# Second-layer memory keys and values moved into the first layer's token-major z products

## The chip, the cores and the metric

The kernel runs on one core of one Trainium2 chip. The metric is the device time of one execution in microseconds (us); lower is better. A core has TensorE (PE: matmuls, and PEld for its weight loads), VectorE (DVE), ScalarE (ACT), GpSimd (POOL) and SyncE (SP), whose queue issues nearly all transfers of this kernel.

## The reference

Two decoder layers over a sequence of 1024 tokens of width 1024, then a final norm. Cut to what matters here:

```python
for l in range(DEPTH):                                   # DEPTH = 2
    h = rms_norm(x, norm_mix_w[l])
    x = x + hybrid_mixer(h, w_in[l], ...)                # one projection of h: q, k, v, gates, z, xbc, dt
    hq = rms_norm(x, norm_xq_w[l])
    mem_n = rms_norm(mem, norm_mem_w[l])                 # mem: 256 tokens, the same for both layers
    x = x + memory_cross_attention(hq, mem_n, w_mq[l], w_mk[l], w_mv[l], w_mo[l])
return rms_norm(x, final_norm_w)

# memory_cross_attention:
k = (mem_n @ wk).reshape(b, m, 4, 256)
v = (mem_n @ wv).reshape(b, m, 4, 256)
```

The keys and values of the memory depend on `mem` and on weights alone, not on `x`. They can be computed at any time before the cross-attention of their layer, which comes at the end of that layer.

## The kernel before

Activations lie feature-major in SBUF: `hhi` and `hlo` hold the normed input as 8 tiles of 128 features by 1024 tokens. Every fp32 operand is split into a high part (a rounded copy, made on ACT by `hi`, L77) and a low part (the rest, made by `lo`, L85, on DVE or POOL). A product is three matmuls, high by high, low by high and high by low (`mm3`, L111 to L113).

The order of PE's instructions is written by hand: PE executes them in the order in which the Python code emits them. The order on the other engines and in SP's queue of transfers is chosen when the program is built, from a model of times and with program order as priority; each queue is then executed in its order. `weave(main, fill)` (L297) emits two generators alternately. A generator yields its modelled PE time as a float; a tuple `(t,)` means "nothing of mine is to be emitted before model time t", and `weave` then emits `fill` until that time, as long as `fill` has anything left. `ratio` says how much of `fill` goes with each step of `main`; at 0.0 `fill` goes into the tuples alone.

The program begins in `start`. It computes memory keys and values of layer 0, `memkv(0)`, and of layer 1, `memkv(1)`, as the `fill` of `norms()`, which norms the memory and the 1024 tokens of x in two halves of 512. Each `memkv` is 8 key tiles (8 k-steps of three matmuls with 256 columns) and 4 pieces of values (2 token chunks of 8 such k-steps): 384 matmuls. Its weights come through `wload`, which loads 128x512 pieces and splits them, into two sets of buffers: `wp` (names `wst`, `whi`, `wlo`, five pieces) and the local pool `n0` (names `xst`, `xhi`, `xlo`, three pieces). `alt_w` decides whether every second low part is made on DVE or all of them on POOL. Results are scaled (`kf`), split (`kh`, `kl`) and stored to DRAM.

The norm of a half is a chain: 8 loads `xt`, squares on ACT (`nsq`), sums on DVE (`nac`, L265), 8 small matmuls that sum over partitions (L221), the reciprocal root (`nms`, `nrs` on POOL, `nrp`, `ndg`), two matmuls that spread it over partitions (L251), a copy `nrr`, and then 8 products `ntm` (L270, DVE) that are split into `hhi` and `hlo`. The eight `xt` buffers are reused by the second half, and `ntm` has three buffers.

What is left of `fill` after the norms is run in `tokmaj` as `first`, ahead of the token-major products: pieces 0 and 1 (v and small gates: `values(0)` for tokens of the first half, `values(1)` for those of the second), then `gate_z`: pieces 2, 3 and 4 (z), 8 token chunks each, woven into `gates`. A piece's weights are loaded in four pairs of k-tiles (`tms`, three buffers), and split on ACT (`tmh`) and POOL (`tml`). Its matmuls are L372 to L374. The pool `tm` with these buffers is opened on the right side of SBUF after the pool `n1` of the norms (`xt`, `nsq`, `nac`, `nrr`, `ntm`, `ndg`, `wn`) was closed there, so its buffers take over addresses of those tiles, and a buffer is first written when the old tiles under it have been read for the last time. After `tokmaj` comes `mixer`, whose first projection loads its weights (`in_w_fm`) through `wp` too.

Of the kernel before, what the change touches and what calls it, by code (L numbers as in the profile page):

```python
# [8 lines left out]
F32 = mybir.dt.float32  # L9
F32R = mybir.dt.float32r  # L10
# [6 lines left out]
P = 128  # L17
# [3 lines left out]
KT = D // P  # L21
NB = T // P
HALF = 512
MT = 256
# [19 lines left out]
class Net:  # L44
# [300 lines left out]
    def tokmaj(self, l, pools, first, norm):  # L345
        nc = self.nc
        mm = nc.tensor.matmul
        W = max(PIECES)
        with self.pool("tm", 2, side="right") as pool:
            self.fdt = self.tile(pool, [P, NB, 24], F32, "fdt", 1)  # L350
            ws = {}
# [44 lines left out]
            def values(half):  # L396
                for pc in range(2):
                    for c in range(4 * half, 4 * half + 4):
                        yield from run(pc, c)

            def gate_z():
                for pc in range(2, len(PIECES)):
                    load(pc)
                    for c in range(NB):
                        yield from run(pc, c)
# [7 lines left out]
            if l == 0:  # L413
                self.fixed_rows()
            self.run(values(1))
            self.weave(self.gates(l), gate_z())


    def gates(self, l):
# [769 lines left out]
    def memnorm(self, pool, tmp):  # L1189
        nc = self.nc  # L1190
        mt = self.mt
        nch = MT // P
        sums = []
        for k in range(0, KT, 2):
            sq = [self.tile(tmp, [P, MT], F32, "msq", 8) for _ in range(2)]
            nc.scalar.activation(sq[0], mt[:, k, :], AF.Square)
            nc.gpsimd.tensor_tensor(out=sq[1], in0=mt[:, k + 1, :], in1=mt[:, k + 1, :], op=ALU.mult)
            nc.vector.tensor_tensor(out=sq[0], in0=sq[0], in1=sq[1], op=ALU.add)
            sums.append(sq[0])
        ps = self.tp()  # L1200
        for c in range(nch):
            for k, sq in enumerate(sums):
                nc.tensor.matmul(
                    ps[:, c : c + 1], sq[:, c * P : (c + 1) * P], self.onecol, start=k == 0, stop=k == len(sums) - 1
                )
        self.mrr = yield from self.spread(tmp, ps, nch, self.tile(pool, [P, MT], F32, "mrr", 1))
        self.mrs = self.const("mrs", [P, nch])
        nc.vector.tensor_copy(self.mrs, self.rs[:, :nch])

    def memw(self, l, pool):  # L1210
        w = self.mw[l]
        if l == 0:

            nhi, nlo = (h[:, :, HALF : HALF + MT] for h in (self.hhi, self.hlo))
        else:
            nhi, nlo = (self.tile(pool, [P, KT, MT], F32R, n, 1) for n in ("nhi", "nlo"))
        for k in range(KT):
            self.hi(nhi[:, k, :], self.mt[:, k, :], w[:, k : k + 1])
            self.lo(nlo[:, k, :], self.mt[:, k, :], nhi[:, k, :], w[:, k : k + 1])
        return nhi, nlo  # L1220


    def memkv(self, l, pool, w0):
        nc, a = self.nc, self.a
        mm = nc.tensor.matmul
        nhi, nlo = self.memw(l, pool) if l == 0 else self.mnext
        todo = []

        def acc(i):
            return self.acc() if i % 2 else self.big()  # L1230

        def keys(t, ps):
            kf = self.tile(pool, [P, MT], F32, "kf")
            nc.vector.tensor_tensor(out=kf, in0=ps, in1=self.mrr, op=ALU.mult)
            kh = self.tile(pool, [P, MT], F32R, "kh")
            kl = self.tile(pool, [P, MT], F32R, "kl")
            self.hi(kh, kf)
            self.lo(kl, kf, kh, eng=nc.gpsimd)
            self.dma(self.kDs[l][0][:, t, :], kh)
            self.dma(self.kDs[l][1][:, t, :], kl)  # L1240

        def values(pc, c, ps):
            r = self.mrs[:, c : c + 1]
            vh = self.tile(pool, [P, MT], F32R, "kh")
            vl = self.tile(pool, [P, MT], F32R, "kl")
            self.hi(vh, ps, r)
            self.lo(vl, ps, vh, r)
            self.dma(self.mvDs[l][0][:, c, pc * MT : (pc + 1) * MT], vh)
            self.dma(self.mvDs[l][1][:, c, pc * MT : (pc + 1) * MT], vl)
# [5 lines left out]
                g(*b)  # L1255

        for t in range(KT):
            ws = w0[t] if t < len(w0) else self.wload(a["w_mk"][l, t], (None, pool)[t % 2])
            ps = acc(t)[:, :MT]
            for k in range(KT):  # L1260
                whi, wlo = ws[k // 4]
                s = slice((k % 4) * P, (k % 4 + 1) * P)
                self.mm3(ps, whi[:, s], wlo[:, s], nhi[:, k, :], nlo[:, k, :], k == 0, k == KT - 1)
                yield 0.33
            put(keys, t, ps)
# [3 lines left out]
        for pc in range(4):  # L1269
            ws = self.wload(a["w_mv"][l, pc, 0]) + self.wload(a["w_mv"][l, pc, 1], pool)  # L1270
            for c in range(2):
                ps = acc(c)[:, :MT]
# [221 lines left out]
    def start(self):  # L1494
        a = self.a
        pools, xp = ExitStack(), ExitStack()
        pool = pools.enter_context(self.pool("n0", 2))
        xp_ = xp.enter_context(self.pool("n1", 2, side="right"))
        self.nb = 3
# [2 lines left out]
        nc = self.nc  # L1502
        nc.scalar.dma_start(self.mw[0], a["norm_mem_w"][0])
        w0 = [self.wload(a["w_mk"][0, 0], first=self.mt[:, 0:2, :])]
# [23 lines left out]
                yield from self.norm_half(xp_, xs, accs, wn, half)  # L1528

        self.ratio = 0.0  # L1530
        fill = chain(self.memkv(0, pool, w0), self.memkv(1, pool, []))
        self.weave(norms(), fill, drain=False)
        xp.close()
        return pools, fill, iter(())
# [84 lines left out]
```

## Time and profile before

| what | value |
|---|---|
| time, median of 3 runs | 2637.05 us (2633.95 to 2640.07) |
| the profiled execution, its own time | 2644.48 us |
| its span | 2642.7 us |
| PE busy | 2527.8 us, 96% of the span |
| DVE, ACT, POOL busy | 1590.9, 1219.2, 1085.6 us |
| mean granted clock of PE | 0.981 |
| share of the chain that ended last | PE 76%, DVE 9%, DMA 5% |

The page of the profile cuts the span in 40 slices of 66 us. These are the digits of busy time in tenths, and what the transfers moved:

```profile
PE   8799999999999988999999999999999998899997
PEclk9899999999999999999999999999999999999999
DMA  7673232222323745454364222222322465445333
GB/s 239 213 228 96 69 91 67 81 79 84 87 79 103 255 157 168 144 167 122 122 195 122 73 77 84 87 73 75 98 73 76 130 240 167 143 156 164 123 95 129
```

The first two slices are where PE has its lowest digits at the front of the program, and the first three where the transfers are densest. A row of the timeline reads: start in us, duration in us, engine, line, operation, output and inputs, shapes, and in brackets the idle time before it with what ended that. Durations of single matmuls overlap, since matmuls are pipelined; the pace is the distance from start to start.

### The profile page before, as it was taken

How to read it: one execution, taken by the hardware profiler on the slowest of the kernel's cores; microseconds unless marked ns; L12 is line 12 of the kernel's file. 1: busy time of each engine (PE TensorE's matmuls, PEld its weight loads, DVE VectorE, ACT ScalarE, POOL GpSimd, SP SyncE). 2: the span in 40 equal slices, each digit the busy share in tenths (PEclk: the TensorE clock that was granted, in tenths of full speed). 3: DMA queues.
4: the chain of work that ended last, by engine and by line, in shares of the span. 5: the costliest groups of instructions: out<-in, count | busy, mean ns of one | idle time of the engine just before them, and what ended most of it. 6: DMA issues, size and time to landing. Idle time of an engine off the chain costs nothing.

```text
span 2642.7 us, 39668 instructions
## 1 busy us (share of the span) xinstructions
PE 2527.8 (96%) x13900; PEld 2098.6 (79%) x13900; DVE 1590.9 (60%) x2940; ACT 1219.2 (46%) x2615; POOL 1085.6 (41%) x1081
## 2 busy tenths in 40 slices
PE   8799999999999988999999999999999998899997
PEld 7799988888777766778879988888877766577886
DVE  6823266666688666663464236666678867665445
ACT  5532254554466545534443135455455644443442
POOL 5642244444455544332252124344354555433233
PEclk9899999999999999999999999999999999999999
DMA  7673232222323745454364222222322465445333
GB/s 239 213 228 96 69 91 67 81 79 84 87 79 103 255 157 168 144 167 122 122 195 122 73 77 84 87 73 75 98 73 76 130 240 167 143 156 164 123 95 129
DMA packets 230363, 332.36 MB, mean 126 GB/s; under 512 B 24626, under 2 KB 107698, under 8 KB 230148
## 3 DMA queue, kind: packets, MB, share of 16 engines
q1 hardware_dynamic: 228292, 327.72, 39.9%
q8 instruction: 110, 1.80, 0.3%
q10 hardware_dynamic: 1872, 2.10, 0.2%
q14 instruction: 89, 0.73, 0.1%
HBM read 237.68 MB, written 86.81 MB: 123 GB/s over the span
## 4 chain that ended last, share of the span: by engine, by line
PE 76%; DVE 9%; DMA 5%; issue 3%; ACT 3%; POOL 2%; SPq 1%; DVEq 0%; ACTq 0%; POOLq 0%
PE acc L111 15%; PE acc L112 14%; PE acc L113 14%; PE tp L667 3%; PE tp L630 2%; PE big L372 2%; PE acc L372 2%; PE acc L374 2%; PE big L374 2%; PE acc L373 2%; PE big L373 2%; PE S L770 1%; PE big L598 1%; PE big L599 1%; PE tp L798 1%
## 5 line engine op out<-in xcount | busy, mean ns | idle before, releaser
L111 PE MATMUL acc<-hhi,whi 128*128 128x512 f32 (+1 forms) x1960 | 801.2, 409 | 2.4 <-DVE xt L1423 1.2
L113 PE MATMUL acc<-hlo,whi 128*128 128x512 f32 (+1 forms) x1960 | 771.9, 394 | 0.0
L112 PE MATMUL acc<-hhi,wlo 128*128 128x512 f32 (+1 forms) x1960 | 770.9, 393 | 0.0
L85 POOL TENSOR_TENSOR wlo<-wst,whi 128x512 fp32r<-128x512 f32 x279 | 376.8, 1351 | 402.3 <-ACT whi L77 337.1
L113 PEld LDWEIGHTS acc<-hlo,whi 128*128 128x128 f32 x1960 | 371.6, 190 | 82.0
L111 PEld LDWEIGHTS acc<-hhi,whi 128*128 128x128 f32 x1960 | 373.8, 191 | 69.6 <-issue 1.6
L112 PEld LDWEIGHTS acc<-hhi,wlo 128*128 128x128 f32 x1960 | 373.1, 190 | 58.0
L77 ACT CAST whi<-wst 128x512 fp32r<-128x512 f32 x420 | 259.5, 618 | 298.8 <-PE acc L113 196.3
L77 ACT CAST ph<-tp 128x512 fp32r<-128x512 f32 (+1 forms) x256 | 142.3, 556 | 180.6 <-PE tp L630 114.2
L85 DVE TENSOR_TENSOR pl<-tp,ph 128x512 fp32r<-128x512 f32 (+1 forms) x256 | 167.2, 653 | 80.1 <-ACT ph L77 78.0
L85 DVE TENSOR_TENSOR wlo<-wst,whi 128x512 fp32r<-128x512 f32 x141 | 114.1, 809 | 117.2 <-ACT whi L77 115.3
L609 POOL TENSOR_SCALAR Pt<-Pt,sm 128x128 f32<-128x128 f32 (+7 forms) x128 | 105.3, 823 | 189.6 <-DVE sm L608 187.5
L1011 DVE SCALAR_TENSOR_TENSOR ac<-u,cw,ac 128x512 f32<-128x512 f32 x144 | 129.1, 896 | 32.4 <-POOL ac L1006 31.0
L607 ACT ACTIVATE Pt<-big,sm 128x128 f32<-128x128 f32 (+7 forms) x128 | 95.0, 743 | 71.6 <-DVE sm L605 64.1
L85 POOL TENSOR_TENSOR tml<-tms,tmh 128x684 fp32r<-128x684 f32 (+3 forms) x40 | 67.8, 1714 | 134.3 <-ACT tmh L77 125.3
L604 DVE TENSOR_REDUCE sm<-big 128x1 f32<-128x128 f32 (+7 forms) x128 | 96.2, 752 | 23.4 <-PE big L601 21.9
L787 POOL TENSOR_TENSOR Pt<-Pt,mx 128x512 f32<-128x512 f32 x64 | 69.4, 1086 | 87.3 <-DVE mx L786 37.2
L372 PE MATMUL big<-tmh,hhi 128*128 128x342 f32 (+3 forms) x320 | 102.0, 319 | 1.0 <-DVE vt L85 1.0
L372 PE MATMUL acc<-tmh,hhi 128*128 128x342 f32 (+3 forms) x320 | 102.1, 319 | 0.0
L374 PE MATMUL acc<-tmh,hlo 128*128 128x342 f32 (+3 forms) x320 | 101.4, 317 | 0.0
L373 PE MATMUL big<-tml,hhi 128*128 128x342 f32 (+3 forms) x320 | 101.4, 317 | 0.0
L374 PE MATMUL big<-tmh,hlo 128*128 128x342 f32 (+3 forms) x320 | 101.4, 317 | 0.0
(338 smaller groups left out, 5242.1 us busy)
## 6 DMA issues: line engine op xcount, KB each, us to landing
wst<-in_w_fm_dram SPq DMA_DIRECT2D x132, 256.0 KB
wst<-in_w_out_dram SPq DMA_DIRECT2D x128, 256.0 KB
wst<-in_w_mq_dram SPq DMA_DIRECT2D x64, 256.0 KB
wst<-in_w_mo_dram SPq DMA_DIRECT2D x64, 256.0 KB
xt<-x_st SPq DMA_DIRECT2D x48, 256.0 KB
v_st<-vt SPq DMA_DIRECT2D x32, 320.0 KB
vs<-v_st SPq DMA_DIRECT2D x20, 512.0 KB
xs_st<-tr SPq DMA_DIRECT2D x40, 256.0 KB
```

Source lines behind the costliest of these rows:

```text
L77: self.nc.scalar.copy(out, in_)
L85: (eng or self.nc.vector).tensor_tensor(out=out, in0=in_, in1=f(hi), op=ALU.subtract)
L111: mm(ps, ahi, bhi, start=first, stop=False)
L112: mm(ps, alo, bhi, start=False, stop=False)
L113: mm(ps, ahi, blo, start=False, stop=last)
L372: mm(ps[:, :n], self.hhi[:, k, cs], hi[:, k, :n], start=k == 0, stop=False)
L373: mm(ps[:, :n], self.hhi[:, k, cs], lo[:, k, :n], start=False, stop=False)
L374: mm(ps[:, :n], self.hlo[:, k, cs], hi[:, k, :n], start=False, stop=k == KT - 1)
L604: nc.vector.tensor_reduce(out=sm[:, 0:1], in_=S[:, :n], axis=AX.X, op=ALU.max)
L607: nc.scalar.activation(Pt[:, :n], S[:, :n], AF.Exp, bias=sm[:, 1:2], scale=1.0, accum_out=sm[:, 2:3])
L609: nc.gpsimd.tensor_scalar(out=Pt[:, :n], in0=Pt[:, :n], scalar1=sm[:, 3:4], scalar2=1.0, op0=ALU.mult, op1=ALU.mult)
L1011: nc.vector.scalar_tensor_tensor(ac, u[:, 5 + j : 5 + j + HALF], w[:, t, j : j + 1], ac, ALU.mult, ALU.add)
```

## The change

The `fill` of `start` is `memkv(0)` alone. `memkv(1)` is emitted in `tokmaj` of layer 0, after `gates`: `gates` is woven with `gate_z` as before, but what is left of `gate_z` is kept, and then `memkv(1)` is woven with it at ratio 1.0, so that equal shares of modelled time alternate; the rest of `gate_z` follows. For this the tiles that `memkv(1)` needs (the split memory `nhi` and `nlo`, the scales `mrr`, the buffers `kf`, `kh`, `kl`) move into a pool `n2` that stays open until then. `memkv(1)` gets no local pool for weights: all its pieces go through `wp`, and since `alt_w` is False at that point, POOL makes all its low parts. The split of the memory for layer 1 (`memw(1)`) stays where it was, inside `memkv(0)`. A scratch area in SBUF is set to 1024 bytes, which makes room. Layer 1's `tokmaj` is as before.

```diff
@@ tokmaj
             self.run(values(1))
-            self.weave(self.gates(l), gate_z())
+            fill = gate_z()
+            self.weave(self.gates(l), fill, drain=l > 0)
+            if l == 0:
+                self.ratio = 1.0
+                self.weave(self.memkv(1, None, []), fill)
+                self.kvp.close()
@@ memnorm
-        self.mrr = yield from self.spread(tmp, ps, nch, self.tile(pool, [P, MT], F32, "mrr", 1))
+        self.mrr = yield from self.spread(tmp, ps, nch, self.tile(self.kp, [P, MT], F32, "mrr", 1))
@@ memw
-            nhi, nlo = (self.tile(pool, [P, KT, MT], F32R, n, 1) for n in ("nhi", "nlo"))
+            nhi, nlo = (self.tile(self.kp, [P, KT, MT], F32R, n, 1) for n in ("nhi", "nlo"))
@@ memkv
-            kf = self.tile(pool, [P, MT], F32, "kf")
+            kf = self.tile(self.kp, [P, MT], F32, "kf")
...
-            ws = w0[t] if t < len(w0) else self.wload(a["w_mk"][l, t], (None, pool)[t % 2])
+            ws = w0[t] if t < len(w0) else self.wload(a["w_mk"][l, t], pool if t % 2 else None)
@@ start
+        self.kvp = ExitStack()
+        kp = self.kp = self.kvp.enter_context(self.pool("n2", 2))
...
-        fill = chain(self.memkv(0, pool, w0), self.memkv(1, pool, []))
+        fill = self.memkv(0, pool, w0)
@@ kernel
-    nc = _bacc.Bacc("TRN2", target_bir_lowering=False, num_devices=1)
+    nc = _bacc.Bacc("TRN2", target_bir_lowering=False, num_devices=1, dynamic_dma_scratch_size=1024)
```

More of the change, by code (lines that the diff above doesn't have):

```diff
@@ L1232, in keys @@
         def keys(t, ps):
-            kf = self.tile(pool, [P, MT], F32, "kf")
+            kf = self.tile(self.kp, [P, MT], F32, "kf")
             nc.vector.tensor_tensor(out=kf, in0=ps, in1=self.mrr, op=ALU.mult)
-            kh = self.tile(pool, [P, MT], F32R, "kh")
-            kl = self.tile(pool, [P, MT], F32R, "kl")
+            kh = self.tile(self.kp, [P, MT], F32R, "kh")
+            kl = self.tile(self.kp, [P, MT], F32R, "kl")
             self.hi(kh, kf)
@@ L1243, in values @@
             r = self.mrs[:, c : c + 1]
-            vh = self.tile(pool, [P, MT], F32R, "kh")
-            vl = self.tile(pool, [P, MT], F32R, "kl")
+            vh = self.tile(self.kp, [P, MT], F32R, "kh")
+            vl = self.tile(self.kp, [P, MT], F32R, "kl")
             self.hi(vh, ps, r)
```

## The prediction

> **What bounds the kernel now.** I read the page first, then the busy time of each engine by stage, then PE's timeline, its waits, and the engines that feed the norm. The stages are the first layer's memory keys and values (5 to 79.2 us), the second layer's (79.2 to 144.2), and the token-major products (144.2 to 299.0); the last row is the end of these, where the diff puts the moved work. Columns: length, then busy time (count) of PE, PEld, DVE, ACT, POOL, then PE's granted clock, the transfer engines' busy share, GB/s.
>
> ```profile
> span 2642.7 us, 39668 instructions
> PE 2527.8 (96%) x13900; PEld 2098.6 (79%) x13900; DVE 1590.9 (60%) x2940; ACT 1219.2 (46%) x2615; POOL 1085.6 (41%) x1081
> ...
> 5.00:79.20 74.20, 64.65 (x413) 62.56 (x414) 53.97 (x80) 43.59 (x90) 40.50 (x35) 0.91 0.76 244
> 79.20:144.20 65.00, 53.03 (x396) 51.76 (x395) 51.20 (x60) 36.41 (x68) 49.06 (x35) 0.89 0.72 220
> 144.20:299.00 154.80, 153.75 (x1001) 152.18 (x1000) 41.90 (x79) 33.05 (x72) 29.50 (x19) 1.00 0.43 127
> 182.00:299.00 117.00, 116.91 (x759) 115.62 (x760) 35.76 (x69) 26.59 (x56) 19.98 (x12) 1.00 0.31 94
> ```
>
> The kernel as a whole is PE's. The stage that the diff takes away is not: in its 65.0 us DVE and POOL are nearly as busy as PE, and PE's clock is down to 0.89. The stage that receives the work is PE alone, 116.91 of 117.00 us, with the transfers at 0.31. So the change moves PE work from a place where it has company to one where PE has no gap. What matters is what the work was worth in the old place. PE's timeline gives the pace and the borders:
>
> ```profile
> 28.63 0.28 PE L111 MATMUL big<-hhi,whi 128*128 128x256 f32 x1
> 34.34 0.28 PE L111 MATMUL big<-hhi,whi 128*128 128x256 f32 x1
> 79.19 0.28 PE L111 MATMUL big<-nhi,whi 128*128 128x256 f32 x1
> 144.20 0.32 PE L372 MATMUL big<-tmh,hhi 128*128 128x344 f32 x1
> 298.96 0.40 PE L111 MATMUL acc<-hhi,whi 128*128 128x512 f32 x1
> ```
>
> The first two rows are two key tiles apart, 48 matmuls: 5.71/48 = 0.119 us each. The 384 matmuls of `memkv(1)` are 384 x 0.119 = 45.7 us at full pace. From 79.19 to 144.20 PE took 65.0 us for them, so 65.0 - 45.7 = 19.3 us went to waits, to a slow clock and to the norm's own matmuls. These waits, in that stretch (total, times, longest):
>
> ```profile
> PE big L1278 <- DVE xlo L85: 6.4, 2, 4.5
> PE tp L221 <- DVE nac L265: 3.4, 1, 3.4
> PE acc L112 <- DVE xlo L85: 1.7, 2, 1.4
> ```
>
> The norm's matmuls of the second half of x, and the first and last of DVE's small operations between the same two matmuls of the first half:
>
> ```profile
> 99.68 1.84 PE L221 MATMUL tp<-onecol,nac 128*128 128x1 f32 x8 [3.40 <-DVE nac L265]
> 108.89 0.62 PE L251 MATMUL tp<-ndg,ones 128*128 128x512 f32 x2
> 59.04 0.15 DVE L232 TENSOR_SCALAR nms<-tp 128x4 f32<-128x4 f32 x1
> 62.90 0.68 DVE L242 TENSOR_TENSOR ndg<-ident,nrp 128x512 fp32r<-128x512 f32 x1
> ```
>
> **The change part by part.** *Removed at the front: 65.0 us between 79.2 and 144.2.* But that stretch did two things. PE's order is fixed, and the norm of the second half of x is emitted into it: its sum (L221) at 99.68 and its spreading (L251) at 108.89. `memkv(0)` holds 42.2 us of modelled time (128 steps of 0.33), and the tuples of the norms ask for some 60 (3 + 5.4, then twice 9.6 + 7 + 3 + 0.8 + 5.4), so the fill runs out while the second half's loads are emitted. PE then comes to L221 right after 79.2 and waits there, then at L251, then at the first token-major product. I follow that chain link by link.
>
> *Up to L221.* The first `ntm` of half 1 frees the `xt` buffers that half 2 loads into; that part is the same, since the splits of `memkv(1)` begin after it. Then DVE was full. Its groups from 77.0 to 99.6 us:
>
> ```profile
> L265 DVE TENSOR_TENSOR nac<-nac,nsq 128x512 f32<-128x512 f32 x7 | 8.2, 1170 | 0.0
> L85 DVE TENSOR_TENSOR wlo<-wst,whi 128x512 fp32r<-128x512 f32 x4 | 4.9, 1223 | 0.0
> L85 DVE TENSOR_TENSOR hlo<-ntm,hhi 128x512 fp32r<-128x512 f32 x3 | 4.2, 1412 | 0.0
> L85 DVE TENSOR_TENSOR xlo<-xst,xhi 128x512 fp32r<-128x512 f32 x3 | 2.0, 678 | 0.0
> L1234 DVE TENSOR_TENSOR kf<-big,mrr 128x256 f32<-128x256 f32 x2 | 0.8, 411 | 0.0
> L1234 DVE TENSOR_TENSOR kf<-acc,mrr 128x256 f32<-128x256 f32 x2 | 0.8, 410 | 0.0
> ```
>
> The `wlo`, `xlo` and `kf` are those of `memkv(1)`: 4.9 + 2.0 + 1.6 = 8.5 us gone, so L221 comes at 91.2 at the latest. The same 128x512 shape took 678 ns in one group and 1170 or 1412 in others; with POOL's `memkv(1)` work gone too, 7 x 0.49 + 3 x 0.73 = 5.6 us more can go: 85.6 at the earliest. I take 88.0.
>
> The Trainium skill, page "SBUF — State Buffer", section "Who interferes with whom", says that a DVE instruction with two inputs in SBUF contends with a GpSimd instruction that reads SBUF, and that the second to issue is blocked until the first is done. The spread of 678 to 1412 ns agrees with it. By it alone the early end, 85.6, would hold, and the sum below would be 2.4 us less.
>
> *L221 to the end of L251.* Half 2 took 108.89 + 0.62 - 99.68 = 9.8 us. In half 1 the part on DVE and POOL took 62.90 + 0.68 - 59.04 = 4.5, and with L221 and L251 around it 1.84 + 4.5 + 0.62 = 7.0. I take 8.0, nearer to half 1, as the queues are emptier: L251 ends at 96.0.
>
> *The products `ntm`, which the weights of the token-major products wait for.* First and last `ntm` of the second half, SP's loads and POOL's `tml`, from the timeline:
>
> ```profile
> 111.10 2.87 DVE L270 SCALAR_TENSOR_TENSOR ntm<-xt,wn,nrr 128x512 f32<-128x512 f32 x3 [1.01 <-ACT nrr L255]
> 126.74 0.74 DVE L270 SCALAR_TENSOR_TENSOR ntm<-xt,wn,nrr 128x512 f32<-128x512 f32 x1
> 124.58 0.33 SPq L72 DMA_DIRECT2D wst<-in_w_fm_dram  x1
> 129.29 1.42 SPq L72 DMA_DIRECT2D tms<-in_w_tm_dram  x3
> 135.47 3.31 POOL L85 TENSOR_TENSOR tml<-tms,tmh 128x688 fp32r<-128x688 f32 x2
> 143.35 1.66 POOL L85 TENSOR_TENSOR tml<-tms,tmh 128x688 fp32r<-128x688 f32 x1
> ```
>
> The buffers of `tm` lie over those of the norms. By the trace, too: SP issued the first three `tms` loads together at 129.29, 1.8 us after the last `ntm` (126.74 + 0.74 = 127.48), although loads of the mixer's weights, later in the program, had gone at 124.58.
>
> From the end of L251 (109.51) to the first `ntm`: 1.6 us. The eight `ntm`: 127.48 - 111.10 = 16.4 us, with splits of `memkv(1)` between them; alone, 8 x 0.74 and four low parts of 0.68 on DVE are 8.6. I take 11.5, since POOL makes the other four low parts in the same chain. From the last `ntm` to the end of the fourth `tml` (143.35 + 1.66 = 145.01): 145.01 - 127.48 = 17.5 us, under a queue full of stores and other splits; four `tml` back to back (3.31/2 each) would be 6.6, if the loads had come early. I take 12.0, the middle. The fourth `tml` then ends at 96.0 + 1.6 + 11.5 + 12.0 = 121.1.
>
> *The start of the token-major products.* In before all of this was covered: the fourth `tml` ended at 145.01, and the first chunk, which uses that pair last, ran from 144.20 without a gap. Uncovered, the first chunk (24 matmuls, 154.8 us for 960 and a few more, so 0.16 each, 3.8 us) is fed pair by pair and ends about 1.0 us after the fourth `tml`. That is as if the stage started at full pace at 121.1 + 1.0 - 3.8 = 118.3.
>
> *The clock.* PE will have stood for most of 79 to 118 us.
>
> ```profile
> 105.16 0.35 PE L113 MATMUL acc<-nlo,xhi 128*128 128x256 f32 x1
> 126.87 0.58 PE L1278 MATMUL big<-xlo,nhi 128*128 128x256 f32 x1 [4.55 <-DVE xlo L85]
> ```
>
> After the wait of 3.40 us at L221, matmuls were slow until 105.16; after the wait of 4.55, the 125 matmuls from 126.87 to 144.20 took 17.33 us instead of 125 x 0.119 = 14.9. I charge these 2.4 us: the stage starts, in effect, at 120.7.
>
> The Trainium skill, page "TensorE: Matmul & The Clock Gate", section "What's actually happening", has half clock after an idle window of about 3.4 us and full clock after about 3.4 us of work. The rows agree that such waits cost clock, but the slow stretch after 99.68 lasted 5.5 us. By the page the charge would be an estimated 1.7 us in place of 2.4.
>
> *Added in the token-major stage: 45.7 us*, in full, since PE had no gap there. `gates` takes 16 + 3 x 1.2 = 19.6 us of the 82 modelled us of `gate_z`; 62 are left for the 42.2 of `memkv(1)`, so all of it is woven one to one and some 20 us of products follow. These cover the mixer's first weights, whose buffers in `wp` are now busy until then. If that cover failed, the four pieces of the first two projections would cost four POOL splits, 5.4 us.
>
> *Waits inside the weave.* Every one of the 32 pieces is split on POOL now:
>
> ```profile
> L85 POOL TENSOR_TENSOR wlo<-wst,whi 128x512 fp32r<-128x512 f32 x279 | 376.8, 1351 | 402.3 <-ACT whi L77 337.1
> L77 ACT CAST whi<-wst 128x512 fp32r<-128x512 f32 x420 | 259.5, 618 | 298.8 <-PE acc L113 196.3
> ```
>
> 32 x 1.35 = 43.2 us of POOL in the roughly 91 us that the weave lasts, ACT 32 x 0.62 = 19.8. A piece is used up in 2 x 45.7/32 = 2.9 us, against 1.35 on POOL: it keeps up. But five buffers hold little more than one piece of values (four), and the `tml` of `gate_z` (four of 1.7 in a row) stand in the same queue, and SP's queue holds stores of keys, values and z between the loads: a load behind a store that waits for its result waits with it. Below: 0, as the stage had no wait. Above: 8.1 us, the waits for low parts of `memkv(1)` in its old place (6.4 + 1.7), where the pace was double. I take 3.
>
> The transfers of `memkv(1)`, loads and stores, now fall into a stretch with a share of 0.31 instead of 0.72; nothing on PE waits there for transfers, so I count no gain.
>
> **Sum.** The stage starts 144.2 - 120.7 = 23.5 us sooner and is 45.7 + 3 longer: +25.2 us. Against the profiled execution (2644.48 us, of which 2642.7 is the span) that is 2669.7; I carry the difference over to the median, 7.4 us lower: 2637.05 + 25.2 = 2662. In words: 65 us of old stage did 45.7 us of work and hid a chain of 41.5 us (79.2 to 120.7); the change pays for both.
>
> Bounds by the low ends: 85.6 + 7.0 + 1.6 + 8.6 + 6.6 + 1.0 - 3.8 = 106.6 and no clock loss, so -37.6 + 45.7 = +8.1, 2645. By the high ends: 91.2 + 9.8 + 1.6 + 16.4 + 17.5 + 1.0 - 3.8 + 2.4 = 136.1, so -8.1 + 45.7 + 8.1 = +45.7, 2683.
>
> **The rivals.** *No change:* the token-major weights don't wait for the last `ntm`, because the scheduler places `tms` and `tml` where the tiles below are done with. The stage could then start at L251's end, 96.0, with the clock's 2.4: 144.2 - 98.4 = 45.8, against 45.7, so 2637 to 2640. For it: the tiles that lie lowest are done early. Against it: the three loads at 129.29.
>
> *Faster:* the weights are early as in that case, and the second half's sum is through at once. With L221 at 85.6, L251 ends at 92.6, and the products start, with no clock loss and no wait in the weave, 51.6 us sooner: -51.6 + 45.7 = -5.9, 2631. It decides from a start before 144.2 - 45.7 = 98.5, and shows from 93.2. Against it: three low ends have to meet.
>
> *Slower still:* the weave starves. If PE stands before each of the four pieces of values for as long as its longest wait here, 4.55 us, that is 18 us where I have 3: 2677, and clock besides. Against it: half the pace, and POOL less than full.
>
> **Chances.** My forecast 0.62; the weave starves 0.13; no change 0.13; faster 0.12. A measurement of this kernel can tell about 0.2%, 5.3 us, from no change. Faster by more 0.12, within 0.13, slower 0.75. The forecast's own range is 2645 to 2683; the one given takes in the case of no change and leaves out the faster one: 2634 to 2684.
>
> **What would show it.** Right: PE idle after about 79 us with L221 near 88 and L251 near 95, waiting for DVE; the first token-major product after 110, waiting for POOL's `tml` or a `tms` load; the first chunk in four steps; DVE's 128x512 operations near 0.7 us in that time; `memkv(1)` woven between 190 and 300 at 0.119 us a matmul; the mixer's first projection near 324 instead of 298.96. Wrong: a first token-major product before 98, or waits of more than 8 us in the weave, or a gap of several us before the mixer.

## The result, and the profile after

| | time, median (lowest to highest) |
|---|---|
| before, on the same chip | 2638.07 us (2633.95 to 2640.07) |
| after | 2663.14 us (2662.26 to 2664.25) |

The ratio is 1.0097, with a 95% interval of 1.008 to 1.0115: the change costs 25.1 us, some 1%, clear of noise. The prediction was 2662, slower. The profiled execution of after took 2662.26 us with a span of 2660.1. The two spans differ by 17.4 only, because the profiled execution of before was 6.4 over its median. So the stage borders are read from the traces, and totals from the medians.

The head of the page of after, and its 40 slices:

```profile
PE 2524.4 (95%) x13900; PEld 2096.1 (79%) x13900; DVE 1564.5 (59%) x2924; ACT 1222.0 (46%) x2615; POOL 1101.9 (41%) x1097
...
PE   8499999999999988999999999999999999899997
...
PEclk9699999999999999999999999999999999999999
```

PE did the same 13900 matmuls in about the same busy time (2524.4 us, before 2527.8). The second slice fell from 7 to 4, and its clock from 9 to 6; from the third on PE is at 9. The hole is new and lies between 66 and 133 us. By stage (columns as in the prediction), with PE's waits from 76 to 324 us:

```profile
79.20:118.10 38.90, 3.69 (x15) 2.61 (x14) 24.50 (x33) 11.89 (x22) 12.68 (x9) 0.53 0.53 146
118.10:323.45 205.35, 202.93 (x1383) 200.62 (x1384) 43.62 (x92) 60.47 (x121) 79.74 (x63) 0.98 0.48 141
```

```profile
PE big L372 <- ACT tmh L77: 18.9, 1, 18.9
PE tp L221 <- DVE nac L265: 14.0, 1, 14.0
PE tp L251 <- DVE ndg L242: 2.3, 1, 2.3
PE big L373 <- POOL tml L85: 1.5, 2, 1.2
PE big L372 <- DVE gar L85: 1.0, 1, 1.0
```

For 38.9 us PE did 3.69 us of work. Its idle time is the norm's chain in three waits: for the sum (L221), for the spreading (L251), and for the first split weights. After that it waits twice for `tml`, 1.5 us together, and once in the weave, 0.96 us for a gate, where before had 1.05 at its only gap. PE's timeline:

```profile
93.64 1.84 PE L221 MATMUL tp<-onecol,nac 128*128 128x1 f32 x8 [13.98 <-DVE nac L265]
97.82 1.40 PE L251 MATMUL tp<-ndg,ones 128*128 128x512 f32 x2 [2.35 <-DVE ndg L242]
...
118.10 0.65 PE L372 MATMUL big<-tmh,hhi 128*128 128x344 f32 x1 [18.88 <-ACT tmh L77]
...
122.30 0.65 PE L373 MATMUL big<-tml,hhi 128*128 128x344 f32 x1 [0.26 <-POOL tml L85]
...
130.54 0.32 PE L372 MATMUL big<-tmh,hhi 128*128 128x344 f32 x1
...
323.45 0.40 PE L111 MATMUL acc<-hhi,whi 128*128 128x512 f32 x1
```

The row at 130.54 is the 49th token-major product, so 48 are behind it. The same product of before:

```profile
151.75 0.32 PE L372 MATMUL big<-tmh,hhi 128*128 128x344 f32 x1
```

In before these 48 ran without a gap from 144.20: 7.55 us, 0.157 each. After's stage began, in effect, at 130.54 - 7.55 = 123.0, which is 21.2 us sooner. From there to the mixer's first projection it took 323.45 - 123.0 = 200.45 us, against 298.96 - 144.20 = 154.76: 45.7 longer, to the tenth the 384 matmuls at full pace. -21.2 + 45.7 = +24.5 at the mixer, +25.1 in the medians.

So the frame of the prediction holds. What it did not have is what else moved into the hole. DVE, SP, ACT and POOL in after:

```profile
82.66 0.91 DVE L207 MEMSET zero<- 128x1024 f32 x1 [0.16 <-issue]
...
99.87 2.08 DVE L270 SCALAR_TENSOR_TENSOR ntm<-xt,wn,nrr 128x512 f32<-128x512 f32 x3 [1.51 <-ACT nrr L255]
...
115.99 0.74 DVE L270 SCALAR_TENSOR_TENSOR ntm<-xt,wn,nrr 128x512 f32<-128x512 f32 x1
```

```profile
87.81 0.40 SPq L72 DMA_DIRECT2D xt<-in_xT_dram  x1
88.26 2.70 SPq L72 DMA_DIRECT2D sr_st<-zero  x4
...
94.70 5.28 SPq L72 DMA_DIRECT2D sr_st<-indr  x4
100.14 2.48 SPq L72 DMA_DIRECT2D gbias<-in_fdt_bias_dram  x1
102.67 2.63 SPq L72 DMA_DIRECT2D gslow<-in_slow_dram  x1
105.33 0.43 SPq L72 DMA_DIRECT2D gan<-in_a_log_dram  x1
105.87 14.38 SPq L72 DMA_DIRECT2D tms<-in_w_tm_dram  x4
```

```profile
92.14 0.63 ACT L264 ACTIVATE nsq<-xt 128x512 f32<-128x512 f32 x1 [2.52 <-DMA xt<-in_xT_dram]
...
107.58 0.21 ACT L477 ACTIVATE gan<-gan 128x16 f32<-128x16 f32 x1 [7.74 <-DMA gan<-in_a_log_dram]
```

```profile
120.59 4.91 POOL L85 TENSOR_TENSOR tml<-tms,tmh 128x688 fp32r<-128x688 f32 x3 [0.69 <-ACT tmh L77]
```

`zero`, `sl_st`, `sr_st`, `indr` belong to `fixed_rows` (constant rows for the mixer, L196); `gbias`, `gslow` and `gan` (the parameter `a_log`) are small loads of `gates`. In program order all stand behind the norms. In before they came late, as DVE's timeline shows for `zero` (`gbias` was issued at 178.56):

```profile
148.54 0.91 DVE L207 MEMSET zero<- 128x1024 f32 x1 [0.16 <-issue]
```

In after they are 60 to 80 us earlier, placed into the time in which PE waits. Stores go between and around the last two `xt` loads, so that the last `xt` takes 4.33 us from its issue (87.81) to its square (92.14), and ahead of the `a_log` load, for which ACT then waits 7.74 us at the very point where `hhi` of the second half is to be made. The likely reason why they come so early, argued and not shown, is that their tiles lie over buffers of the front that `memkv(1)` held in before.

The row of the four `tms` loads hides a wait. This is SP's longest from 80 to 130 us:

```profile
SPq L72 <- DVE ntm L270: 10.5, 1, 10.5
```

The first load went at 105.87; the second waited for the last `ntm`, which ended at 116.73. The first pair's `tmh` came on ACT behind the last split of `ntm`. So the weights do wait for the last `ntm`, as the prediction has it.

### The profile page after: what moved, and what is told of

Same layout as the page of the kernel before. It is cut to its first block, busy times and chain, and to the rows that moved or that the text cites. A ratio compares the mean times of both kernels' runs of the same rounds, so it can differ in the third digit from the quotient of the medians.

```text
span 2660.1 us, 39653 instructions
## 1 busy us (share of the span) xinstructions
PE 2524.4 (95%) x13900; PEld 2096.1 (79%) x13900; DVE 1564.5 (59%) x2924; ACT 1222.0 (46%) x2615; POOL 1101.9 (41%) x1097
## 4 chain that ended last, share of the span: by engine, by line
PE 76%; DVE 9%; DMA 5%; issue 4%; ACT 3%; POOL 2%; SPq 1%; DVEq 0%; ACTq 0%; POOLq 0%
PE acc L111 15%; PE acc L113 14%; PE acc L112 14%; PE tp L672 3%; PE tp L635 2%; PE big L372 2%; PE big L373 2%; PE big L374 2%; PE acc L372 2%; PE acc L374 2%; PE acc L373 2%; SPq L72 1%; PE S L775 1%; PE big L603 1%; PE big L604 1%
## 5 line engine op out<-in xcount | busy, mean ns | idle before, releaser
L85 POOL TENSOR_TENSOR wlo<-wst,whi 128x512 fp32r<-128x512 f32 x303 | 407.0, 1345 | 451.8 <-ACT whi L77 379.2
L77 ACT CAST whi<-wst 128x512 fp32r<-128x512 f32 x436 | 269.5, 618 | 313.5 <-PE acc L113 200.2
L85 DVE TENSOR_TENSOR wlo<-wst,whi 128x512 fp32r<-128x512 f32 x133 | 104.3, 784 | 113.1 <-ACT whi L77 111.3
L372 PE MATMUL big<-tmh,hhi 128*128 128x342 f32 (+3 forms) x320 | 103.3, 323 | 19.8 <-ACT tmh L77 18.9
L609 DVE TENSOR_REDUCE sm<-big 128x1 f32<-128x128 f32 (+7 forms) x128 | 96.2, 751 | 23.9 <-PE big L606 22.3
L374 PE MATMUL big<-tmh,hlo 128*128 128x342 f32 (+3 forms) x320 | 102.4, 320 | 0.0
```

The lines of the kernel that those rows point to most:

```text
L77: self.nc.scalar.copy(out, in_)
L85: (eng or self.nc.vector).tensor_tensor(out=out, in0=in_, in1=f(hi), op=ALU.subtract)
L372: mm(ps[:, :n], self.hhi[:, k, cs], hi[:, k, :n], start=k == 0, stop=False)
L374: mm(ps[:, :n], self.hlo[:, k, cs], hi[:, k, :n], start=False, stop=k == KT - 1)
L609: nc.vector.tensor_reduce(out=sm[:, 0:1], in_=S[:, :n], axis=AX.X, op=ALU.max)
```

## The experiments

The last column is the difference of medians to the kernel before, run in the same group on one chip. Line numbers shift a little with the edits. The 49th product is the mark of the row at 130.54 above. There is no run e9.

The columns of borders are of one execution each, and these differ before the change comes into play. The first column is the start of the spreading (L251) of the first half of x. Up to there every kernel but e6, e7 and e8 runs the queues of before (from e4 on with the early `a_log` load), and yet it came at 61.4 to 67.3 us. Where that matters, borders below are counted from it. From the mixer to the end the traces took another 2336.7 to 2348.0 us, so that borders and medians can differ by several us.

| kernel | half 1's L251 starts | L251 ends | 49th product | mixer begins | median, us | ratio (95%) | to before |
|---|---|---|---|---|---|---|---|
| before | 66.8 | 109.5 | 151.8 | 298.96 | 2638.07 | | |
| after | 67.3 | 99.2 | 130.5 | 323.45 | 2663.14 | 1.0097 (1.008 to 1.0115) | +25.1 |
| e1 second layer's keys and values left out | 63.3 | 97.0 | 127.9 | 273.80 | 2622.24 | 0.9932 (0.9916 to 0.9948) | -16.9 |
| e2 keys at the front | 65.5 | 108.7 | 152.2 | 322.28 | 2670.54 | 1.0109 (1.0091 to 1.0128) | +31.4 |
| e3 zeros after the norm | 61.4 | 91.1 | 123.1 | 316.01 | 2664.38 | 1.0092 (1.0077 to 1.0107) | +25.3 |
| e4 `a_log` early | 64.2 | 96.9 | 121.8 | 314.77 | 2657.54 | 1.0064 (1.005 to 1.0079) | +18.4 |
| e5 e4, fixed rows last | 65.4 | 94.8 | 119.2 | 326.39 | 2671.86 | 1.0119 (1.0104 to 1.0134) | +32.2 |
| e6 e5, own buffers for piece 0 | 73.2 | 102.4 | 111.1 | 315.54 | 2658.53 | 1.0069 (1.0055 to 1.0084) | +18.8 |
| e7 e5, 16 `xt` buffers | 70.7 | 92.2 | 116.7 | 324.24 | 2667.45 | 1.0101 (1.0085 to 1.0117) | +27.8 |
| e8 e6, keys at the front | 74.5 | 118.7 | 128.2 | 312.17 | 2652.86 | 1.0048 (1.0033 to 1.0063) | +13.2 |
| e10 e4, fixed rows after chunk 0 | 66.3 | 95.8 | 120.3 | 313.19 | 2654.61 | 1.0066 (1.0051 to 1.0081) | +16.8 |
| e11 e10, own buffers, loads tied | 65.5 | 100.9 | 109.6 | 311.23 | 2657.64 | 1.0072 (1.0056 to 1.0088) | +19.9 |
| e12 e11, keys at the front | 66.9 | 111.7 | 121.4 | 304.58 | 2648.41 | 1.004 (1.0028 to 1.0053) | +10.6 |
| e13 e12, piece by piece | 62.0 | 107.5 | 118.2 | 296.48 | 2644.73 | 1.0021 (1.0011 to 1.003) | +6.6 |

**e1: what the work is worth in each place.**

```diff
-                self.weave(self.memkv(1, None, []), fill)
+                self.run(fill)
-                    self.dma(kt, self.kDs[l][s][:, 2 * h : 2 * h + 2, :])
+                    self.dma(kt, self.kDs[0][s][:, 2 * h : 2 * h + 2, :])
```

> The changed kernel without memkv(1) at all: the second layer's keys and values are not computed, and the second layer's attention reads those of the first. It prices the same work in both places: before minus this is what memkv(1) cost at the front, after minus this what it costs in the z products. Theory (at the front 65 us of stage did 45.7 us of work and hid a chain that now stands bare, in the z products PE has no gap): this is 45.7 + 1 us under after, 2616.4 us, so the price was 22 us in the old place and is 47 in the new. Rival 1 (the weave is dear: one set of five weight buffers, POOL alone for low parts): 52 us or more under after, below 2611. Rival 2 (the z products hide part of the work, and the loss sits elsewhere): 40 us or less under after, above 2623.

PE's timeline in e1, the 49th product:

```profile
127.91 0.32 PE L372 MATMUL big<-tmh,hhi 128*128 128x344 f32 x1
```

From the effective start (127.91 - 7.55 = 120.36) e1's stage took 153.4 us, after's 200.45: in the new place the work costs 47.0, all of its 45.7 us and 1.3 more. In the old place it cost 298.96 - 273.80 = 25.2 by the traces, of which 3.4 stand already at half 1's L251, so 21.7; by the medians it is 16.9. Both say that the old place hid 24 to 29 us of it. By the medians the new place costs 25.1 + 16.9 = 42.0. So the theory's two prices, 22 and 47, are those of the traces, but its time of 2616.4 was 5.8 us too low, and the second rival's bound, 2623, is near. In the z products themselves the traces show nothing hidden; where the 5 us between 47.0 and 42.0 lie is open.

**e4 and e3: the two things in the way.** e4 loads `a_log` in the set-up; e3 makes the zeros from the second half's last normed tile, so that their stores can't go before the norm is done.

```diff
# e4
+        self.an0 = const("an0", [P, 16])
+        self.dma(self.an0, a["a_log"][0])
...
-            an = self.load_w(pool, a["a_log"][l], 16, "gan")
+            an = self.an0 if l == 0 else self.load_w(pool, a["a_log"][l], 16, "gan")
# e3
-            nc.vector.memset(f(zero), 0.0)
+            nc.vector.tensor_scalar(out=zero, in0=f(self.hhi[:, KT - 1, :]), scalar1=0.0, scalar2=None, op0=ALU.mult)
```

> The changed kernel with layer 0's a_log loaded in setup into a tile of its own; its exponential stays where it is in the program. Theory (ACT's queue had that exponential ahead of the split of the first ntm and waited 7.7 us for its load): the last ntm ends near 109 instead of 116.7, the products start 7 us sooner: 2656. Rival (the loads of the token-major weights are the bound, as SP issued the first only at 105.9 behind the stores of the fixed rows): the wait moves from ACT to the load, as after, 2663.

> The changed kernel, with the zero fill of fixed_rows made from the last normed tile times 0.0 instead of a memset, so that it and its stores (some 3 MB) can't start before the second half is normed. Theory (the fixed rows moved up into the norm's time, and their stores held up the loads of x and of a_log in SP's queue and DVE by 3.3 us): L221 from 93.6 to near 88, the chain from there shorter too: 6 to 13 us under after, 2650 to 2657. Rival (the stores only fill idle transfer time, the chain is bound by DVE, POOL and ACT): as after, 2663.

DVE's last `ntm` in e4:

```profile
107.11 0.74 DVE L272 SCALAR_TENSOR_TENSOR ntm<-xt,wn,nrr 128x512 f32<-128x512 f32 x1
```

The eight `ntm` end 10.9 us after L251 in e4 and 17.5 in after (115.99 + 0.74 - 99.22): 6.6 us, the medians 25.1 - 18.4 = 6.7. So the `a_log` load alone is 6.7 of the 25.1 us. In e3 the norm passed sooner. These are the spreading of half 1 and the sum of half 2, on PE:

```profile
61.41 1.05 PE L251 MATMUL tp<-ndg,ones 128*128 128x512 f32 x2
...
85.54 1.83 PE L221 MATMUL tp<-onecol,nac 128*128 128x1 f32 x8 [11.48 <-DVE nac L265]
```

From the first to the second it took 24.1 us, and 23.9 to 24.2 in e5, e10 and e11 below, where the zeros come late too. With the zeros in the way it took 26.3 (after), 28.1 (e1) and 27.2 (e4). So the zeros and their stores cost 2 to 4 us of the chain; the last `xt` took 4.3 us from issue to square in those three, and 2.6 to 2.7 in e3, e5 and e10. But in e3 six of the stores then went ahead of the fourth pair of weights in SP's queue (from 106.17, the load at 110.25).

Its mixer began 7.4 us sooner than after's in the profiled execution, which was the shortest of its runs, but 5.9 of these stand already at half 1's L251; its median is 0.2 further from before than after's. In e3 the `a_log` load moved too, to 128.6 behind the norm, and the eight `ntm` took 10.3 us as in e4; what the chain gained by both was lost again at the weights.

**e2: half of the work at the front.** The keys back at the front, the values in the weave.

```diff
-                self.weave(self.memkv(1, None, []), fill)
+                self.weave(self.memkv(1, None, [], "v"), fill)
-        fill = self.memkv(0, pool, w0)
+        fill = chain(self.memkv(0, pool, w0), self.memkv(1, pool, [], "k"))
```

> Half of the change undone: the keys of memkv(1) are computed at the front again, its values stay in the z products. Theory (what has to be covered is the whole chain up to the low parts of the first token-major weights, 22 us from the end of L251 to the stage's effective start): L251 near 109 as in before, the token-major products start in effect near 131.5 us, the 192 matmuls of the values add 22.9: +11 us on before, 2649. Rival (only the wait up to L251 is bare, the weights would be there in time): the products start right after the keys, near 112 us: -10 us, 2628.

Both were wrong. L251 ended at 108.7, and the keys covered the norm as expected, but the weights were late: PE waited 21.1 us for the first pair and 5.74 for the fourth. SP's queue, and PE:

```profile
129.28 6.09 SPq L72 DMA_DIRECT2D sr_st<-indr  x4
135.47 2.18 SPq L72 DMA_DIRECT2D tms<-in_w_tm_dram  x1
```

```profile
143.71 0.66 PE L372 MATMUL big<-tmh,hhi 128*128 128x344 f32 x1 [5.74 <-ACT tmh L77]
```

The fixed rows' stores stand in the middle of the weights' loads, and PE waits for the fourth pair.

**e5, e6, e7, e8: the stores last, and buffers that overlie nothing.** In e5 the zeros depend on the last chunk of the first piece, and `fixed_rows` follows `values(1)`. e6 adds buffers (`t0h`, `t0l`, `t0s`) for piece 0 in a pool of their own; e7 instead gives `xt` 16 buffers; e8 is e6 with the keys at the front.

```diff
# e5
+            self.run(values(1))
             if l == 0:
                 self.fixed_rows()
-            self.run(values(1))
-            nc.vector.memset(f(zero), 0.0)
+            nc.vector.tensor_scalar(
+                out=zero, in0=f(self.hhi[:, KT - 1, :]), scalar1=self.fdt[:, NB - 1, 0:1], scalar2=0.0,
...
# e6
+                own = l == 0 and pc == 0
+                wp = self.t0 if own else pool
+                hi = self.tile(wp, [P, KT, W], F32R, "t0h" if own else "tmh")
# e7
-                    xt = self.tile(xp_, [P, HALF], F32, "xt", 8)
+                    xt = self.tile(xp_, [P, HALF], F32, "xt", 16)
```

> The changed kernel with the early load of a_log and with fixed_rows emitted after values(1) and tied to its last result, so that neither its small operations nor its stores stand in a queue during the norm and the first weights. Theory (the bare chain was lengthened by strangers in the queues of ACT and SP): the wait at L221 falls to about 11.5 us, the ntm take 10.3, the first two chunks end near 114 us instead of 121.8 with a_log alone: 13 us under after, 2650. Rival (the stores of the fixed rows only move, and hold up the loads and stores of the z products instead): the gain is given back before the mixer, 2657.

> As e5, and the weights of piece 0 get buffers that lie over nothing of the norms (the pool n0 is closed before tm opens, to make the room). Theory (the first products wait for weights only because their buffers lie over tiles that the last ntm reads): they start at the end of L251, some 13 us before e5's, and their 15 us cover the ntm and piece 1's weights: 2637, as before. Rival (the wait moves to piece 1, whose weights still come after the last ntm): 5 us under e5, 2645.

> As e5, with 16 buffers xt instead of 8, so that the loads, squares and sums of the second half need not wait for the first half's ntm. Theory (the wait at L221 is the turn-round of the xt buffers): L221 right behind the last product of memkv(0), 9 us under e5, 2641. Rival (DVE has to do both halves' sums, ntm and low parts anyway and is the bound up to L251): 3 us under e5 or less, 2647.

> As e6, and the keys of memkv(1) are computed at the front again, its values in the z products. Theory (the chain up to L251 has to be covered by work that PE has to do anyway, and no more work than that belongs there): the keys cover L221 and L251 as in before (L251 near 109), piece 0 starts right behind them near 111 and covers the ntm, the values add 22.9 us in the weave: 111 - 144.2 + 22.9 + 1 = -9 us on before, 2629. Rival (DVE and POOL, full at the front with keys and norms together, keep PE waiting as before): no gain on before, 2637 to 2642.

e5's 49th product came at 119.2, 11.3 us before after's, but only 2.6 before e4's (3.8 counted from half 1's L251), where some 114 was expected. The edit took the zeros and the stores out of the norm; `oner` and `indr` still ran on DVE at 79.6 and 84.9. Then PE's timeline:

```profile
200.08 1.24 PE L465 MATMUL big<-triu,glf 128*8 128x128 f32 x5 [12.05 <-DVE glf L457]
```

On SP the load of the gates' bias is now issued at 185.33 (it takes 0.49), behind the same stores (the last of them at 173.31 to 179.43), and PE waits 12.05 us for the gates. The gain was turned into a new wait, and the time, 2671.9, lies beyond the rival's 2657. e6 shows the overlaid buffers; PE's timeline there:

```profile
101.04 1.40 PE L256 MATMUL tp<-ndg,ones 128*128 128x512 f32 x2 [2.34 <-DVE ndg L247]
102.24 0.49 PE L383 MATMUL big<-t0h,hhi 128*128 128x344 f32 x1
```

With buffers of its own the first product follows L251 without a wait; in e5 it came 12.3 us behind. But the loads went at 23 to 35 us and took time from `memkv(0)`: L251 ended 7.6 us later than in e5 (half 1's L251 came at 73.2 already), and both expected times were missed. e7's rival came nearer: with all `xt` there, L221 came at 81.1 without a wait, but L251 waited 8.8 for DVE and its end moved by 2.6 only; the median fell by 4.4. In e8 the early loads and the keys together put L251 at 118.7, and a gates wait of 6.0 stayed: 2652.9 where 2629, or 2637 to 2642 by the rival, was expected.

**e10 to e13: one cover after another.** e10 is e4 with the zeros tied to the first chunk of the first piece. e11 adds e6's buffers, and the first three of their four loads each wait for a small write that reads the first half's last normed tile. e12 puts the keys at the front. e13 takes piece 0 for all eight chunks, then piece 1.

```diff
# e10
-            nc.vector.memset(f(zero), 0.0)
+            nc.vector.tensor_scalar(
+                out=zero, in0=f(self.hhi[:, KT - 1, :]), scalar1=self.fdt[:, 0, 0:1], scalar2=0.0,
...
# e11
+                    if own and k < 6:
+                        nc.vector.tensor_copy(st[:, 0, 0:1], f(self.hhi[:, KT - 1, 0:1]))
                     self.dma(st[:, :, :n], src[:, k : k + 2, :])
# e13
+                if l == 0:
+                    for c in range(NB):
+                        yield from run(half, c)
+                    return
```

> The changed kernel, with the first layer's a_log loaded in the set-up, and with the block of zeros from which the fixed rows' stores are fed made out of the first transposed chunk of the small gates' inputs (times zero). So those stores can't go before that chunk, which stands after the weights' loads of the first piece and ahead of the gates. Theory (the fixed rows' work and the a_log load stand in the way of the norm and of the weights; what followed in the kernel that had them after the second piece was only that the gates' bias load came behind their stores): the 48th token-major product at about 119 us as there, no wait of more than 2 us at the gates, the mixer's first projection at about 312.5 us, 11 before the changed kernel's, time about 2652. Rival (wherever the stores go, a load that PE needs stands behind them): a wait of 5 us or more at the gates or at a second piece's weights, 2660 or more.

> As the kernel before it in this list, and the first piece of token-major weights has buffers of its own, which lie over nothing of the norms; each of its loads waits for a small write that reads the first half's last normed tile, so that it can't go ahead of the layer's memory keys and values. Theory (the 41.5 us that the chain of the second half takes from the end of the memory's keys and values to the first product are the norm, some 17 us, and the rest the waiting of the weights for buffers that overlie the norms'): memory values end at about 79 us, L251 at about 96, the products begin right there at full pace, the mixer's first projection at about 298.5, time about 2638, no change against before. Rival (the weights' loads and splits take DVE, POOL and transfer time out of the norm chain, which ends 5 us or more later, or the gates wait): 2645 or more.

> As the kernel before it in this list, with the second layer's keys computed at the front again, behind the first layer's values, and only its values in the weave. Theory (the norm's chain needs some 17 to 25 us of cover on PE, and the keys are 22.9 us of PE work that need no more than that): products in effect from about 110 us, the values 22.9 us in the weave, the mixer's first projection at about 288 us, time about 2628, 11 under before. Rival (with the keys' weights and splits at the front DVE, POOL and the transfers are full again and the chain gets longer by what the keys cover): 2640 or more.

> As the kernel with the keys at the front and the first piece's loads tied, but the first layer's token-major products take the first piece for all eight token chunks and then the second piece for all eight, instead of both pieces for the first half of the tokens and then both for the second. There PE needed the second piece's weights from about 129 us, while the last of their low parts, in buffers that overlie the norms', ended at 143.3: products 96 to 192 took 25.0 us where 96 take 14.2 at full pace. Theory (the cover that is still lacking is of these 13 us, counted with the wait before product 96): the first piece lasts until about 144 us, product 192 at about 143 to 144 instead of 156.0, the mixer's first projection at about 292, time 13 lower, 2635, some 3 us or 0.1% under before. Rival (the products of the second half's tokens wait instead, for the second half's normed tiles, or the second piece waits all the same, since its buffers come free later): mixer's projection at 299 or later, time 2642 or more.

e10 did what was expected (313.2 at the mixer for 312.5, 2654.6 for 2652), without a wait at the gates. Beside e4 it is 3.7 us sooner at the mixer, counted from half 1's L251, and nearly all of that lies ahead of L221 (23.9 for 27.2); from L251 to the 49th product it took 24.5 against 24.9. By the medians it is only 1.6 us, from different groups of runs, which is not clear of their noise.

e11's rival held. The products do follow L251 at once, yet L251 itself was late. PE, DVE and POOL in e11, then DVE in e10:

```profile
99.53 1.40 PE L256 MATMUL tp<-ndg,ones 128*128 128x512 f32 x2 [8.01 <-DVE ndg L247]
100.73 0.49 PE L385 MATMUL big<-t0h,hhi 128*128 128x344 f32 x1
```

```profile
94.16 1.60 DVE L242 CAST nrp<-nrs 128x4 fp32r<-128x4 f32 x1 [2.45 <-POOL nrs L239]
```

```profile
94.10 4.82 POOL L85 TENSOR_TENSOR t0l<-t0s,t0h 128x688 fp32r<-128x688 f32 x3
```

```profile
93.41 0.17 DVE L242 CAST nrp<-nrs 128x4 fp32r<-128x4 f32 x1 [1.12 <-POOL nrs L239]
```

Four numbers a partition took 1.60 us on DVE while POOL split weights in steps of 4.82/3 = 1.61, and 0.17 when POOL was idle. Three such blocks, and `nrs` behind a split on POOL itself, are the 5.7 us by which the wait at L251 grew (8.01 against 2.34 in e10). Piece 1, whose buffers still lie over the norms', then waited, its fourth pair again behind `sr_st<-zero`: products 96 to 192 took 22.8 us for 14.1 at full pace. Of the 10.7 us gained at the 49th product 2.0 were left at the mixer, and the median is 3.0 above e10's.

e12 took 22.9 us of keys out of the weave and paid 11.8 at the 49th product and 4.3 in the next 144: 6.7 net by the trace, 8.0 counted from half 1's L251, 9.2 by the medians. Against its expectation (mixer at 288) it is 16.6 late: 3.9 before the products, 13.0 at piece 1. e13 removed most of that second part: product 192 came at 140.7, but 4.9 of its lead over e12 stand already at half 1's L251, so it is 145.6 by e12's count, where 143 to 144 was expected. Then a new wait came, in PE's timeline and ACT's:

```profile
157.89 0.63 PE L385 MATMUL acc<-tmh,hhi 128*128 128x320 f32 x1 [6.43 <-ACT fdt L400]
```

```profile
156.21 0.43 ACT L77 CAST vt<-acc 128x320 fp32r<-128x320 f32 x1 [10.50 <-DMA v_st<-vt]
```

ACT waited for the store of an earlier `vt`, issued behind the four `sr_st<-indr` stores. e13 ended at +6.6 us (it was expected to be 3 under before), and no version beat before. Its mixer began 2.5 us sooner than that of before, but 2.3 later counted from half 1's L251; no run shows where the rest of the 6.6 lies.

## Why the prediction was right

*What the old stage was worth.* Right. It said that 65 us did 45.7 us of work and hid a chain of 41.5. Measured, the chain is 79.66 (L221's start less its wait) to an effective 123.0, 43.3 us.

*The 45.7 us in full.* Right by the traces: +45.7 by the borders, 47.0 against e1. By the medians against e1 it is 42.0.

*The chain, term by term.* Right in its sum, wrong in its parts:

| term | predicted | measured |
|---|---|---|
| L221 of half 2 | 88.0 (85.6 to 91.2) | 93.64 |
| from there to the end of L251 | 8.0 (7.0 to 9.8) | 5.6 |
| to the first `ntm` | 1.6 | 0.65 |
| eight `ntm` | 11.5 (8.6 to 16.4) | 16.9 |
| last `ntm` to the end of the fourth `tml` | 12.0 (6.6 to 17.5) | 8.8 |
| end of the fourth `tml` | 121.1 | 125.5 |
| effective start, clock with it | 120.7 | 123.0 |

L221 lies beyond its bound. The step that failed is the bound itself: "8.5 us gone, so L221 comes at 91.2 at the latest" took away DVE work from the old stretch and let nothing come in. `zero`, `oner` and `indr` came onto DVE, and the stores between the `xt` loads. Counted from half 1's L251 (66.8 in before) the prediction gave L221 21.2 us (18.8 to 24.4); it took 26.3, and 23.9 to 24.2 where the zeros come late (e3, e5, e10, e11), at the upper end of the range. The 8.5 us were also too many by 1.2, since the last of the four `wlo` in them ran beside and behind L221, which started at 99.68, and could not hold it up. From DVE's timeline of before:

```profile
99.46 1.21 DVE L85 TENSOR_TENSOR wlo<-wst,whi 128x512 fp32r<-128x512 f32 x1
```

The `ntm` were long for the `a_log` load; without it (e4) they took 10.3, inside the range and near the 11.5. In the other direction, the queues were emptier than the middle values allowed: L251 followed 5.6 us after L221, below the low bound that was taken from half 1, since `nms` to `ndg` took 2.9 us (95.51 to 98.37) instead of 4.5.

*The clock.* A charge of 2.4 us was too much: PE ran at half pace until 125.9, but in that time the `tml` held it back anyway: it waited for the first two, and the third and fourth ended at about 123.9 and 125.5, when PE at half pace came to them at 124.19 and 125.91. The first chunk's 24 products were through at 126.8, 1.3 us after the fourth `tml`. The prediction had an estimated 1.0 without a clock loss, so the loss cost some 0.3 by that.

*Waits in the weave.* 3 was charged, 0.96 came, against 1.05 at the gap of before: nothing net. POOL was busy 53.4 us of the 98 from 208 to 306 and kept up. The gap before the mixer did not appear.

Net: the start 2.3 us later than predicted, the weave 3 us cheaper. The total of 2662 against 2663.1 is partly a cancellation.

*The rivals.* "No change" and "faster" needed the token-major weights early. They were not: with the overlaid buffers the first product waited 18.9 us, and e6 and e11 show that buffers of their own remove exactly that wait. Even then the kernel stayed slower (+18.8, +19.9): the early loads and splits lengthened the norm's chain (5.7 us at L251 in e11), and piece 1, whose buffers still overlie the norms', waited in its turn (22.8 us for 14.1 in e11). Starving of the weave did not happen.

## What to carry to other kernels

Before moving work out of a stage with idle time, ask what chain that work was covering: the price of work is the stage's time with it less the stage's time without it, not the work's own length, and here 45.7 us of matmuls cost 17 to 22 in one place and 42 to 47 in the other. When a stage is emptied, list what else is ready to run there: in-order queues were filled with stores and small loads that nobody needed yet, and one of them (a load of 8 KB) cost 6.7 us. Removing one wait is worth only the distance to the next one behind it in the same queue (e5, e11, e13); measure it at the following border, not at the wait. And count borders from the last point that the change can't touch: here the same queues reached such a point up to 5.9 us apart in single executions.

## What was not expected of the hardware

*A queue can be slow with few bytes.* In after, the transfers by stretch (last columns: their share and GB/s):

```profile
83.60:94.70 11.10, 1.06 (x6) 1.09 (x6) 8.12 (x12) 3.12 (x5) 2.06 (x1) 0.50 0.88 309
94.70:105.30 10.60, 2.17 (x6) 1.26 (x6) 3.77 (x8) 0.59 (x1) 1.01 (x1) 0.50 0.45 47
```

After the four `sr_st<-indr` stores (128 KB each) SP took 2.48 us to issue a load of 12 KB and 2.63 for one of 64 KB, while 47 GB/s moved; in e5 the same 12 KB load, issued later, took 0.49. Why these stores are slow was not tried.

*A tiny DVE operation can cost a whole POOL operation.* This is the 0.17 against 1.60 us in e11. The Trainium skill, page "SBUF — State Buffer", section "Who interferes with whom", has two-input operations of DVE contend with GpSimd's reads, and casts too where they run in a mode with two ports, the later one being blocked for the whole instruction of the earlier. The rows agree, to the length of POOL's step; the mode of this cast is not shown.

*The slow clock's length.* In e13, after the wait of 6.43 us (PE's clock is the third column from the right; in the next 3.8 us it was 1.00):

```profile
157.89:161.20 3.31, 3.31 (x12) 3.31 (x13) 2.60 (x4) 1.15 (x3) 1.61 (x1) 0.50 0.78 259
```

Half pace for 3.3 us of unbroken work. Where waits for `tml` broke the work, it lasted longer: 7.8 us in after (118.10 to 125.9) and 5.4 in e5 (107.13 to 112.55). It does not simply start anew at each gap. In after the last gap, 0.26 us before 122.30, stands 3.6 us ahead of full pace; in e5 the last gap, 0.23 us before 111.30, only 1.25 us:

```profile
111.30:112.55 1.25, 1.25 (x4) 1.25 (x5) 0.00 (x0) 0.75 (x1) 1.25 (x1) 0.54 0.20 22
112.55:114.50 1.95, 1.60 (x9) 1.12 (x8) 0.00 (x0) 0.08 (x2) 1.94 (x2) 1.00 0.74 173
```

The Trainium skill, page "TensorE: Matmul & The Clock Gate", section "What's actually happening", gives about 3.4 us of sustained work; the unbroken stretch agrees. What sets the length of a broken one is left open.
